# Relative-bias rows made beside the first convolution layer and copied DRAM to DRAM in eight pieces

## The chip, the cores and the metric

The kernel runs on one core of a Trainium2 chip, as one program from the first load to the last store. The metric is the time of one execution on the device in microseconds (us); of several executions the median is taken.

## The reference, cut to what matters

Two blocks are computed one behind the other for 256 tokens of 1024 features. The first block has two layers: a gated recurrence (HGRN) with a convolutional feed-forward layer behind it, then a sparse attention (DSA) with a second convolutional feed-forward layer behind that. The second block (gMLP, a latent attention, SwiGLU layers) is not touched. What the change is about is the bias of the sparse attention, which depends on the distance between a query and a key:

```
def one_block(args):                      # 128 queries at a time
    scores = where(admissible, index_scores(q_idx, k_idx, w_idx), NEG_BIG)
    _, sel = lax.top_k(scores, top_k)     # the 64 best keys of every query
    logits = q . k[sel] * 64 ** -0.5
    rel = q_pos - sel
    bias = rel_bias[t5_causal_bucket(rel)]   # table of 32 buckets by 16 heads
    probs = softmax(where(rel >= 0, logits + bias, NEG_BIG))
    return probs . v[sel]

def conv_ffn(x, w_up, conv_w, conv_b, w_down):
    h = causal_depthwise_conv3(x @ w_up) + conv_b
    gate, up = split(h)
    return (silu(gate) * up) @ w_down
```

The bias needs nothing that the layers compute: it is made of `rel_bias`, an input, and constants.

## The kernel before

All 256 tokens stay on the chip; weights stream in from DRAM. A **unit** of weights is 1024 rows by 256 columns, 1 MB: `fetch` (L210) issues its load on SP's DMA queue into one of 3 buffers `wst`, `unit` (L227) splits it in two parts whose sum it is (ScalarE writes `whi`, VectorE then `wlo`, 4 buffers each), and TensorE multiplies with `feat` or `tok`, three products for each of the 8 blocks of 128 rows. A load can be issued when the VectorE split of the unit three before has read its buffer, a split when TensorE is done with the unit four before. So the weights run ahead of TensorE by up to three split units and three loaded or loading ones.

`conv_ffn` (L666) runs 11 times over a pair of units, one for the gate and one for the up part: TensorE fills a bank `acc` (4 of them), VectorE scales it into `cvx` (2 buffers), ScalarE and VectorE form the convolution in `cvg` and `cvu`, and the product is split into `fh` and `fl`. Then `down` multiplies with `ffn_w_down`, 12 units.

`rel_bias` (L1041) stands behind the first layer's `conv_ffn` in the program. It loads a one-hot matrix `onehot` (distance to bucket) and the table `rtab`, makes one matrix product into a bank `mx`, copies it to `rrow` in SBUF (head by distance, 384 values in each of 16 rows), and writes every row 128 times to `bias_rows` in DRAM, 3 MB in one transfer. `dsa` (L1059) then reads, for 12 steps, a skewed window of it into `dx` (L1163), to which the products of queries and keys are added. Its weights come as one unit for index keys and keys, two for the index queries `dqi`, half a unit for values and four for queries `dq`; index scores (`pr`, L1106, then `drl`, L1109, then `dsc`) and the 64 best keys (L1122, L1123) come ahead of the 12 steps.

What sets the order of the work is a scheduler of the build: instructions are placed on each engine by modelled readiness, unless `behind` ties them to TensorE's last instruction so far. On an engine, and on SP's queue of DMA issues, they then run strictly in the order so found: a wait of one holds all behind it. Buffers of a tag are handed out in program order (`onehot` and `dx` take from the 4 of tag `e`, which `cvg` uses too; `rrow` from the 4 of tag `m`).

Of the kernel before, what the change touches and what calls it, by code (L numbers as in the profile page):

```python
# [15 lines left out]
P = 128  # L16
# [19 lines left out]
# buffers by tag: a tag's tiles are handed out in the order of the program  # L36
# [9 lines left out]
# a step's later parts, in steps behind its first, and the steps before which the queries' products come  # L46
# [7 lines left out]
# V values, N turned latent of the queries, P their rope part, R its rope, Q queries, S scores, T turned, O out  # L54
MLA_ORDER = "N0 V0 N1 V1 V2 P0 P1 Q0 R0 Q1 R1 S0 Q2 S1 T0 Q3 O0 S2 T1 S3 V3 O1 T2 O2 T3 O3"
TURN_OLD, TURN_NEW = (8, 5), (6, 4)
N_HOLD = 3
N_START = 12
# [63 lines left out]
class Feat:  # L122
    """1024 or more features by 256 tokens, two chunks of 128 features to a tile"""
# [14 lines left out]
class Split:  # L138
    """a Feat in two parts, hi and lo, whose sum it is"""
# [8 lines left out]
class Net:  # L148
# [10 lines left out]
    # ---- tiles  # L159
# [32 lines left out]
    def behind(s):  # L192
        """what follows on TensorE is queued behind the last of its instructions so far"""
        pe = mybir.EngineType.PE
        return s.tc.issue_after(next(i for i in reversed(s.nc.cur_bb.bb.instructions) if i.engine == pe))

    def warm(s, n):
        """n products that nobody reads, behind the last of TensorE's instructions so far: its clock halves at rest"""
        if n:
            with s.behind():  # L200
                ps = s.prod()
                x = s.ident.bitcast(BF16)
                for _ in range(n):
                    s.nc.tensor.matmul(ps[:, :T], x[:, :P], x, start=True, stop=True)

    # ---- weights
    def fetch(s, parts, k0, nk, cuts=1):
        """columns of matrices, side by side, for k of 128 rows: on their way"""
# [14 lines left out]
    def begin(s, p, fine=0):  # L223
        """a layer: the first of its weights are split in smaller pieces"""
        s.fine, s.order = fine or N_FINE, list(ORD_POST if s.posted else ORD_RES)
        s.marks = p.marks

    def unit(s, parts, k0, nk, fetched=None):
        """the same, split in two"""
# [13 lines left out]
        with ExitStack() as stack:  # L243
            # behind what the layer waits for
# [10 lines left out]
    def feat(s, w, c, x, ps):  # L255
        """ps[c-th 128 columns of w, tokens] = w^T x over the unit's k."""
# [10 lines left out]
    def feat2(s, w, x, c=0, beside=None):  # L267
        """two chunks of columns in one bank; beside() after each, in this order on TensorE"""
# [11 lines left out]
    def tok(s, w, cols, t, x, ps, ks=None):  # L280
        """ps[tokens of tile t, cols of w] = x^T w over the unit's k."""
# [11 lines left out]
    def tok2(s, w, x, beside=None):  # L293
        """both tiles of tokens by the 256 columns of a unit, in one bank"""
# [8 lines left out]
    def split_scaled(s, parts):  # L303
        """(hi, lo, source, scale) of several chunks: a tile's parts are all written before they are read"""
# [6 lines left out]
    # ---- norms  # L311
    class Sum:
        """squares summed over chunks; the last chunk is left apart"""

    def sumsq(s, sm, src, k, n, scale=None):
# [3 lines left out]
        if k == n - 4:  # L319
            # the table of the square root, ahead of its use  # L320
# [8 lines left out]
    def rsqrt(s, out, ss, n, eps, factor=1.0):  # L329
        """out = factor * (ss / n + eps) ** -0.5 on small tiles."""  # L330
# [14 lines left out]
    def rsqrt_v(s, out, ss, n, eps):  # L345
        """the same on VectorE alone: a first guess from the bits, then Newton's steps"""
# [13 lines left out]
    def colsum(s, sm, st):  # L360
        """per-token sums of feature-major tiles -> [128 tokens, 2] in a bank"""
# [5 lines left out]
    def bcast(s, r, st):  # L367
        """[128 tokens, 2] -> [128, 256] of a bank, the same on all partitions"""
# [12 lines left out]
    class Pre:  # L381
        """the input of a layer, normed and split: x(k). The token's factor is left to its consumer:
        r by token, rb along the free axis"""
# [8 lines left out]
    def pre_group(s, p, n, sums=True, bank=None):  # L392
        """256 features of h, turned and split, and their squares' sums"""
# [13 lines left out]
    def pre_half(s, p, t, m, sums=True):  # L407
        """the same for a half of the features of a tile of tokens"""
# [15 lines left out]
    def squares(s, ss, src, n):  # L424
        """the sums of squares by token of a group of 256 features, src by token tile"""
# [3 lines left out]
        if n == 2:  # L429
            # the table of the square root, ahead of its use  # L430
# [20 lines left out]
    # ---- start  # L451
    def load_vectors(s, g, parts, queue):
        """rows of 128 values -> one column of s.vectors each"""
# [81 lines left out]
    def conv_vectors(s, l):  # L535
        """the taps and biases of a layer's convolution"""
# [7 lines left out]
    # ---- feed-forward layers  # L544
    def down(s, w, hid, kn, out, n_beside=0):
        """out(n, ps) for the 4 groups of 256 columns of hid @ w, hid of kn chunks; ps by token tile"""
# [4 lines left out]
        for n in range(4 - out.late):  # L551
            both = n < n_beside
            if both:
                # the two tiles in one bank, zeroed for both: a chunk of hid serves both at once
# [25 lines left out]
        # the last units: a tile of tokens to its end, then the other  # L580
# [32 lines left out]
    def tok_turn(s, p, units, t, ps, at=()):  # L613
        """both units side by side for a tile of tokens, what p has left to do before the k's in at"""
# [11 lines left out]
    def swiglu(s, p, wg, wu, wd, out, beside=None):  # L626
# [3 lines left out]
        for i in range(KF // 2):  # L630
# [4 lines left out]
            if p.halves and i == 0:  # L635
                # by token: the first tile of tokens is there before the second
# [26 lines left out]
    def conv_ffn(s, p, l, out):  # L663
# [11 lines left out]
        h2 = lambda x: x.rearrange("p (j t) -> p j t", j=2)  # L675
        for i in range(KF // 2):
            if l == 0 and i in (3, 6):
                # those of the next one
                if i == 3:
                    turns = s.conv_vectors(1)  # L680
                else:
                    with s.behind():
                        for turn in turns:
                            turn()
            ys = [s.e("cvg"), s.m("cvu")]
# [28 lines left out]
    # ---- first block, layer 0  # L714
    def hgrn(s, p, first):
# [40 lines left out]
        def decay(pr):  # L756
            """the logarithms, summed from the start of a chunk"""
# [11 lines left out]
            # exp(x - bk) = k exp(x - b)  # L769
# [4 lines left out]
        def query(pr):  # L774
            """without the tokens' factor"""
# [5 lines left out]
        def offsets():  # L781
            """what lies between a chunk of 32 and the border of the two tiles of 128 tokens"""
# [7 lines left out]
            # the same for the 64 tokens at the start of every 128  # L790
# [13 lines left out]
        def gates(pr):  # L804
            """silu(x) = x / 2 * (1 + tanh(x / 2)); x / 2 without the tokens' factor"""
# [9 lines left out]
        def prepare(pr):  # L815
            """the products' place"""
# [6 lines left out]
        def inner(pr):  # L823
# [4 lines left out]
            def blocks(m, B):  # L828
                """B tokens against the B before them, where these begin at a multiple of 2 B"""
# [8 lines left out]
            def diagonal(lv, x, y):  # L838
                """the pairs of 2^lv tokens, (row of the first half, column of the second)"""
# [8 lines left out]
            # chunks of 32 against the borders between them: keys before a border, queries behind it  # L848
# [39 lines left out]
            # within the chunks, against the middle of every 2 B tokens  # L888
# [61 lines left out]
        # the heads' parts, a few at a time beside the halves of the products  # L950
        def parts():
            steps, at = 0, {}
            for pr in range(NP):
                while len(qs) <= pr:
                    yield
                for _ in inner(pr):
                    # the ends of the pairs before, some steps later
# [82 lines left out]
    # ---- first block, layer 1  # L1040
    def rel_bias(s):  # L1041
        """rows of the bias by distance, in DRAM: for head h and query row q of 128, a row whose
        value 127 - q + j is the bias of the key j - 128 behind the block"""
        nc, a = s.nc, s.a
        onehot = s.e("onehot")[:, :384]
        tab = s.tmp("rtab", P)
        nc.sync.dma_start(onehot, a["consts"][:, C_ONEHOT:])
        nc.gpsimd.memset(tab, 0.0)
        nc.gpsimd.memset(tab[32:64], NEG)
        nc.sync.dma_start(tab[:32, :16], a["rel_bias"])  # L1050
        ps = s.mix()
        nc.tensor.matmul(ps[:, :384], tab, onehot, start=True, stop=True)
        row = s.m("rrow")[:, :384]
        nc.vector.tensor_copy(row, ps[:, :384])
        scr = s.dp.tile([16, P, 384], F32, name="bias_rows")
        nc.sync.dma_start(scr, row[:16][:, None, :].to_broadcast([16, P, 384]))
        s.bias_rows = scr

    def dsa(s, p, out_):  # L1059
# [6 lines left out]
        # index keys and weights beside a filler, then the keys of both heads  # L1066
# [706 lines left out]
```

## Time and profile before

| | |
|---|---|
| median of 3 runs | 1662.58 us (1660.65 to 1665.51) |
| span of the profiled execution, first to last instruction | 1657.0 us |
| median less span: what lies around the span | 5.6 us |
| TensorE busy, share of the span | 98% |
| VectorE, ScalarE, GpSimd busy | 69%, 55%, 0% |
| DMA queue of SP: packets' time, share of 16 engines' span | 57.8% |
| HBM read, written | 291.19 MB, 4.19 MB |

The own time of the profiled execution is not listed beside its span; the median stands for it. TensorE's 98% are counted over overlapping matmuls. In the table of 40 slices only one slice of TensorE's granted clock falls below 9 tenths behind the start of the program, the tenth (373 to 414 us), and its busy digit there is 5. Shares of the span are means over stages with different limits, so the rows below are read by stage: the sparse attention's begin (355 to 420 us) and the first convolution layer (180 to 290 us).

### The profile page before, as it was taken

The numbers are of one execution on the slowest core, as the hardware profiler recorded it, in microseconds if no ns is written. First come the engines' busy times: TensorE is split into PE (matmuls) and PEld (weight loads), VectorE is DVE, ScalarE is ACT, GpSimd is POOL, SyncE is SP. The second block draws the span as 40 slices with busy tenths as digits, with TensorE's granted clock in tenths as the row PEclk, the third lists the DMA queues.
The fourth block names the chain that finished last, engine by engine and source line by source line (L and its number), as shares of the span: only waits on it lengthen the run. The fifth ranks groups of instructions, "written<-read, shape, count | busy, mean of one in ns | idle before, by whom it ended". The sixth has DMA issues, their size and how long they took to land.

```text
span 1657.0 us, 34152 instructions
## 1 busy us (share of the span) xinstructions
PE 1619.9 (98%) x14500; PEld 1606.8 (97%) x14502; DVE 1150.6 (69%) x1900; ACT 913.8 (55%) x1443; POOL 6.7 (0%) x28
## 2 busy tenths in 40 slices
PE   8989999995999999999999999999999999999998
PEld 7989999995999999999999999999999999999998
DVE  6986899654859886766667857664686647677653
ACT  7865766453656656544465546444564446665442
POOL 0000000000000000000000000000000000000000
PEclk9999999997999999999999999999999999999999
DMA  8731755678446566566847565556376565447562
GB/s 266 217 100 53 228 188 187 191 154 190 136 136 218 174 202 192 184 192 193 250 144 228 178 191 172 185 171 203 124 241 188 195 201 142 154 133 227 184 202 71
DMA packets 303821, 297.58 MB, mean 180 GB/s; under 512 B 14295, under 2 KB 300214, under 8 KB 303670
## 3 DMA queue, kind: packets, MB, share of 16 engines
q1 hardware_dynamic: 303622, 295.40, 57.8%
q8 instruction: 114, 1.87, 0.5%
q14 instruction: 37, 0.30, 0.1%
q10 hardware_dynamic: 48, 0.01, 0.0%
HBM read 291.19 MB, written 4.19 MB: 178 GB/s over the span
## 4 chain that ended last, share of the span: by engine, by line
PE 91%; DVE 3%; DMA 3%; ACT 2%; issue 1%; SPq 0%; DVEq 0%; ACTq 0%
PE acc L265 16%; PE acc L263 16%; PE acc L264 16%; PE acc L565 8%; PE acc L567 7%; PE acc L566 7%; PE acc L289 3%; PE acc L290 3%; PE acc L291 3%; DMA bias_rows<-rrow 2%; PE acc L576 2%; PE acc L578 2%; PE acc L577 1%; DVE wlo L251 1%; ACT whi L249 1%; PE pr L844 1%
## 5 line engine op out<-in xcount | busy, mean ns | idle before, releaser
L249 ACT ACTIVATE whi<-wst 128x2048 fp32r<-128x2048 f32 (+4 forms) x404 | 524.2, 1331 | 507.1 <-issue 225.3
L251 DVE TENSOR_TENSOR wlo<-wst,whi 128x2048 fp32r<-128x2048 f32 (+4 forms) x404 | 620.9, 1560 | 247.4 <-ACT whi L249 245.6
L263 PE MATMUL acc<-xh,whi 128*128 128x256 f32 x2416 | 671.9, 279 | 1.3 <-ACT xh L306 0.9
L264 PE MATMUL acc<-xl,whi 128*128 128x256 f32 x2416 | 671.8, 279 | 1.0 <-DVE xl L308 1.0
L265 PE MATMUL acc<-xh,wlo 128*128 128x256 f32 x2416 | 671.3, 279 | 0.5 <-DVE wlo L251 0.5
L264 PEld LDWEIGHTS acc<-xl,whi 128*128 128x128 f32 x2416 | 456.1, 189 | 1.7 <-DVE xl L308 1.4
L263 PEld LDWEIGHTS acc<-xh,whi 128*128 128x128 f32 x2416 | 453.4, 188 | 2.0 <-ACT xh L306 1.1
L265 PEld LDWEIGHTS acc<-xh,wlo 128*128 128x128 f32 x2416 | 454.2, 188 | 0.9 <-DVE wlo L251 0.7
L567 PE MATMUL acc<-wlo,fh 128*128 128x256 f32 x880 | 245.0, 279 | 0.0
L566 PE MATMUL acc<-whi,fl 128*128 128x256 f32 x880 | 244.1, 278 | 0.0
L565 PE MATMUL acc<-whi,fh 128*128 128x256 f32 x880 | 244.0, 278 | 0.0
L567 PEld LDWEIGHTS acc<-wlo,fh 128*128 128x128 f32 x880 | 165.2, 188 | 0.0
L566 PEld LDWEIGHTS acc<-whi,fl 128*128 128x128 f32 x880 | 165.1, 188 | 0.0
L565 PEld LDWEIGHTS acc<-whi,fh 128*128 128x128 f32 x880 | 164.9, 188 | 0.0
L289 PE MATMUL acc<-whi,xh 128*128 128x256 f32 x384 | 108.9, 283 | 0.0
L290 PE MATMUL acc<-whi,xl 128*128 128x256 f32 x384 | 107.0, 279 | 0.0
L291 PE MATMUL acc<-wlo,xh 128*128 128x256 f32 x384 | 107.0, 279 | 0.0
L289 PEld LDWEIGHTS acc<-whi,xh 128*128 128x128 f32 x384 | 72.1, 188 | 0.2
L290 PEld LDWEIGHTS acc<-whi,xl 128*128 128x128 f32 x384 | 72.1, 188 | 0.0
L291 PEld LDWEIGHTS acc<-wlo,xh 128*128 128x128 f32 x384 | 72.1, 188 | 0.0
L658 DVE TENSOR_TENSOR ffu<-acc,rb 128x512 f32<-128x512 f32 x41 | 28.3, 690 | 46.5 <-PE acc L265 46.4
L308 DVE SCALAR_TENSOR_TENSOR xl<-mx,vectors,xh 128x128 fp32r<-128x128 f32 (+1 forms) x124 | 39.1, 375 | 22.9 <-ACT xh L306 22.8
(422 smaller groups left out, 2116.6 us busy)
## 6 DMA issues: line engine op xcount, KB each, us to landing
wst<-in_ffn_w_up_dram SPq DMA_DIRECT2D x88, 1024.0 KB, 5.3
wst<-in_ffn_w_down_dram SPq DMA_DIRECT2D x48, 1024.0 KB, 5.4
wst<-in_ffn_w_gate_dram SPq DMA_DIRECT2D x44, 1024.0 KB, 5.4
wst<-in_ffn_w_down_dram SPq DMA_DIRECT2D x24, 768.0 KB, 4.8
wst<-in_gmlp_w_in_dram SPq DMA_DIRECT2D x16, 1024.0 KB, 5.6
wst<-in_hgrn_w_in_dram SPq DMA_DIRECT2D x13, 1024.0 KB, 5.7
wst<-in_gmlp_w_out_dram SPq DMA_DIRECT2D x8, 1024.0 KB
wst<-in_dsa_w_in_dram SPq DMA_DIRECT2D x6, 1024.0 KB
```

What stands on the lines that cost most here:

```text
L249: s.nc.scalar.activation(hi[:, c], w[:, c], AF.Copy)
L251: s.nc.vector.tensor_tensor(lo[:, c], w[:, c], hi[:, c].bitcast(F32), op=OP.subtract)
L263: mm(ps, wh[:, k, cols], xh, start=k == 0, stop=False)
L264: mm(ps, wh[:, k, cols], xl, start=False, stop=False)
L265: mm(ps, wl[:, k, cols], xh, start=False, stop=k == nk - 1)
L289: mm(ps, xh[:, ts], wk, start=k == 0, stop=False)
L290: mm(ps, xl[:, ts], wk, start=False, stop=False)
L291: mm(ps, xh[:, ts], lk, start=False, stop=k == nk - 1)
L308: b = s.nc.vector.scalar_tensor_tensor(lo, src, g, hi.bitcast(F32), op0=OP.mult, op1=OP.subtract)
L565: mm(ps[t], xh, wh[:, k], start=k0 + k == 0 and not both, stop=False)
L566: mm(ps[t], xl, wh[:, k], start=False, stop=False)
L567: mm(ps[t], xh, wl[:, k], start=False, stop=k0 + k == kn - 1 and (t == 1 or not both))
```

## The change

`rel_bias` now returns a list of ten steps instead of running at once, and `conv_ffn` of the first layer takes one of them from the list at each of its passes 1 to 10, ahead of the pass's products. The first step loads `onehot` and `rtab`. The second makes the product, tied behind TensorE's last instruction, copies 16 rows of it to `rrow`, and writes them once to `bias_row` in DRAM (24 KB). The other eight each copy two heads' rows from `bias_row`, 128 times each, to `bias_rows`, DRAM to DRAM (384 KB written). The call behind `conv_ffn` goes. The rest of the file's difference is comments.

```
+N_SPREAD = 2
...
         h2 = lambda x: x.rearrange("p (j t) -> p j t", j=2)
+        bias = s.rel_bias() if l == 0 else []
         for i in range(KF // 2):
...
+            if i and bias:
+                bias.pop(0)()
             ys = [s.e("cvg"), s.m("cvu")]
...
     def rel_bias(s):
         nc, a = s.nc, s.a
-        onehot = s.e("onehot")[:, :384]
-        tab = s.tmp("rtab", P)
-        nc.sync.dma_start(onehot, a["consts"][:, C_ONEHOT:])
-        nc.gpsimd.memset(tab, 0.0)
-        nc.gpsimd.memset(tab[32:64], NEG)
-        nc.sync.dma_start(tab[:32, :16], a["rel_bias"])
-        ps = s.mix()
-        nc.tensor.matmul(ps[:, :384], tab, onehot, start=True, stop=True)
-        row = s.m("rrow")[:, :384]
-        nc.vector.tensor_copy(row, ps[:, :384])
+        flat = s.dp.tile([16, 384], F32, name="bias_row")
         scr = s.dp.tile([16, P, 384], F32, name="bias_rows")
-        nc.sync.dma_start(scr, row[:16][:, None, :].to_broadcast([16, P, 384]))
         s.bias_rows = scr
+        parts = []
+
+        def load():
+            onehot, tab = s.e("onehot")[:, :384], s.tmp("rtab", P)
+            nc.sync.dma_start(onehot, a["consts"][:, C_ONEHOT:])
+            nc.gpsimd.memset(tab, 0.0)
+            nc.gpsimd.memset(tab[32:64], NEG)
+            nc.sync.dma_start(tab[:32, :16], a["rel_bias"])
+            parts.extend((onehot, tab))
+
+        def product():
+            onehot, tab = parts
+            with s.behind():
+                ps = s.mix()
+                nc.tensor.matmul(ps[:, :384], tab, onehot, start=True, stop=True)
+            row = s.m("rrow")[:, :384]
+            nc.vector.tensor_copy(row[:16], ps[:16, :384])
+            nc.sync.dma_start(flat, row[:16])
+
+        def spread(h):
+            nc.sync.dma_start(scr[h:h + N_SPREAD], flat[h:h + N_SPREAD][:, None, :].to_broadcast([N_SPREAD, P, 384]))
+
+        return [load, product] + [lambda h=h: spread(h) for h in range(0, 16, N_SPREAD)]
...
         s.conv_ffn(p, 0, s.residual(nxt))
-        s.rel_bias()
```

Where the scheduler puts this is seen in the built programs. Lines of the changed file have other numbers than those of the file before.

SP's queue of DMA issues, before, from the last weights of the recurrence to the first of `down`:

```order
L216 DMA wst<-in_hgrn_w_out_dram 128x8x256 x4
L216 DMA wst<-in_ffn_w_up_dram 128x8x256 x3
L1050 DMA rtab<-in_rel_bias_dram 32x16
L216 DMA wst<-in_ffn_w_up_dram 128x8x256 x19
L216 DMA wst<-in_ffn_w_down_dram 128x6x256
```

The same queue in the changed kernel, from the fourth unit of `ffn_w_up`:

```order
L218 DMA wst<-in_ffn_w_up_dram 128x8x256 x4
L1057 DMA onehot<-in_consts_dram 128x384
L218 DMA wst<-in_ffn_w_up_dram 128x8x256 x4
L1070 DMA bias_row<-rrow 16x384
L1073 DMA bias_rows<-bias_row 256x1x384 x3
L218 DMA wst<-in_ffn_w_up_dram 128x8x256
L1073 DMA bias_rows<-bias_row 256x1x384 x5
L218 DMA wst<-in_ffn_w_up_dram 128x8x256 x10
```

The eight pieces stand not one to a pass but in two groups, three between the eleventh and the twelfth unit of `ffn_w_up` and five between the twelfth and the thirteenth. The first waits for the landing of `bias_row`.

SP's queue where the sparse attention begins, before:

```order
L216 DMA wst<-in_dsa_w_in_dram 128x8x128
L216 DMA wst<-in_dsa_w_in_dram 128x8x256 x2
L1056 DMA bias_rows<-rrow 2048x1x384
L216 DMA wst<-in_dsa_w_in_dram 128x8x256
L1163 DMA dx<-bias_rows 128x4x128 x4
L216 DMA wst<-in_dsa_w_in_dram 128x8x256
L216 DMA wst<-in_dsa_w_out_dram 128x8x256 x3
```

And now:

```order
L218 DMA wst<-in_dsa_w_in_dram 128x8x128
L218 DMA wst<-in_dsa_w_in_dram 128x8x256 x3
L1181 DMA dx<-bias_rows 128x4x128 x4
L218 DMA wst<-in_dsa_w_in_dram 128x8x256
L218 DMA wst<-in_dsa_w_out_dram 128x8x256 x3
```

The 3 MB transfer is gone from between the query units; the four `dx` loads stand where they stood, ahead of the last query unit.

VectorE in the convolution layer, ahead of the split of the ninth unit of `ffn_w_up` (the `wlo` row), before:

```order
L690 TENSOR_TENSOR cvx<-acc,rb 128x512
L672 SCALAR_TENSOR_TENSOR cvg<-cvx,vectors,cvg 128x255
L673 SCALAR_TENSOR_TENSOR cvg<-cvx,vectors,cvg 128x254
L251 TENSOR_TENSOR wlo<-wst,whi 128x2048
L301 TENSOR_TENSOR fl<-cvu,fh 128x512
```

And now:

```order
L695 TENSOR_TENSOR cvx<-acc,rb 128x512
L674 SCALAR_TENSOR_TENSOR cvg<-cvx,vectors,cvg 128x255
L675 SCALAR_TENSOR_TENSOR cvg<-cvx,vectors,cvg 128x254
L1069 COPY rrow<-mx 16x384
L253 TENSOR_TENSOR wlo<-wst,whi 128x2048
```

The copy to `rrow` has come in just ahead of that split; on TensorE the product stands behind the fourth unit of the layer.

## Rows read from the trace of the kernel before

**Rows 1.** The page: its span, and the chain that ended last by engine.
```profile
span 1657.0 us, 34152 instructions
...
PE 91%; DVE 3%; DMA 3%; ACT 2%; issue 1%; SPq 0%; DVEq 0%; ACTq 0%
```

**Rows 2.** Chain in order of time, 340 to 460 us: start us, us, what.
```profile
355.64 32.54 DMA bias_rows<-rrow
...
390.31 7.64 DMA wst<-in_dsa_w_in_dram
```

**Rows 3.** Timelines of SP, ACT, DVE there: start us, us, instruction, [idle before <-releaser].
```profile
356.41 9.46 SPq L216 DMA_DIRECT2D wst<-in_dsa_w_in_dram  x1
...
391.47 1.91 ACT L249 ACTIVATE whi<-wst 128x2048 fp32r<-128x2048 f32 x1 [20.37 <-DMA wst<-in_dsa_w_in_dram]
...
400.00 2.29 DVE L251 TENSOR_TENSOR wlo<-wst,whi 128x2048 fp32r<-128x2048 f32 x1 [2.88 <-ACT whi L249]
```

**Rows 4.** Stretches: PE, PEld, DVE, ACT, POOL busy us (count), PEclk, DMA share, GB/s.
```profile
377.40:393.70 16.30, 0.28 (x3) 0.07 (x1) 0.29 (x1) 2.23 (x3) 0.00 (x0) 0.58 0.99 188
393.70:397.30 3.60, 3.60 (x17) 3.60 (x18) 3.25 (x5) 0.22 (x1) 0.00 (x0) 0.52 1.11 339
...
405.00:419.20 14.20, 14.15 (x119) 13.73 (x118) 13.82 (x56) 7.91 (x12) 0.00 (x0) 1.00 0.14 48
sum 41.80, PE 24.72 PEld 23.61 DVE 22.19 ACT 14.87 POOL 0.00; mean PE 4.94 PEld 4.72 DVE 4.44 ACT 2.97 POOL 0.00
```

**Rows 5.** Timeline of SP, convolution layer: loads of its eleventh and twelfth units.
```profile
198.04 0.37 SPq L216 DMA_DIRECT2D wst<-in_ffn_w_up_dram  x1
202.62 0.37 SPq L216 DMA_DIRECT2D wst<-in_ffn_w_up_dram  x1
```

**Rows 6.** Timelines of ACT (twelfth, thirteenth unit) and DVE (ninth, twelfth): the splits.
```profile
214.31 1.92 ACT L249 ACTIVATE whi<-wst 128x2048 fp32r<-128x2048 f32 x1
219.75 1.92 ACT L249 ACTIVATE whi<-wst 128x2048 fp32r<-128x2048 f32 x1 [2.54 <-PE acc L264]
...
200.31 2.28 DVE L251 TENSOR_TENSOR wlo<-wst,whi 128x2048 fp32r<-128x2048 f32 x1
...
216.27 2.29 DVE L251 TENSOR_TENSOR wlo<-wst,whi 128x2048 fp32r<-128x2048 f32 x1
```

**Rows 7.** A stretch of the convolution layer, columns as in the stretches above.
```profile
195.00:215.00 20.00, 20.00 (x179) 20.00 (x178) 19.52 (x29) 13.11 (x17) 0.00 (x0) 1.00 0.72 225
```

**Rows 8.** DMA view, 116 to 121 us, one load of a unit; page: units' landing.
```profile
DMA packets 1041, 1.07 MB, mean 213 GB/s; under 512 B 16, under 2 KB 1040, under 8 KB 1040
...
q1 hardware_dynamic: 1040, 1.05, 64.9%
...
wst<-in_ffn_w_up_dram SPq DMA_DIRECT2D x88, 1024.0 KB, 5.3
```

**Rows 9.** DMA view, 1645 to 1657 us: the eight stores of the result, SBUF to DRAM.
```profile
q1 hardware_dynamic: 1152, 1.05, 26.2%
...
out_dram<-h SPq DMA_DIRECT2D x8, 128.0 KB, 1.8
```

**Rows 10.** DMA view, 358 to 387 us: the transfer to bias_rows alone.
```profile
q1 hardware_dynamic: 1934, 2.97, 89.9%
```

**Rows 11.** DMA view, 74 to 81 us: four loads of 44 rows, one unit landing.
```profile
DMA packets 1793, 1.70 MB, mean 243 GB/s; under 512 B 60, under 2 KB 1792, under 8 KB 1792
...
vst<-in_ffn_conv_w_dram SPq DMA_DIRECT2D x3, 22.0 KB
vst<-in_ffn_conv_b_dram SPq DMA_DIRECT2D x1, 22.0 KB
```

**Rows 12.** Page: the queue of ACT's DMAs; DMA view 0 to 2.2 us: its two loads.
```profile
q10 hardware_dynamic: 48, 0.01, 0.0%
...
vst<-in_attn_norm_dram ACTq DMA_DIRECT2D x1, 8.0 KB
vst<-n_hgrn_lower_bounds_dram ACTq DMA_DIRECT2D x1, 4.0 KB
```

More of the change, by code (lines that the diff above doesn't have):

```diff
@@ L312 @@
     class Sum:
+        pass
     def sumsq(s, sm, src, k, n, scale=None):
@@ L381 @@
     class Pre:
+        pass
     def pre(s, gain):
```

## The prediction

> **What bounds the kernel now.** The first view is the page with its chain of the work that ended last: 91% of the span is TensorE, 3% (some 50 us) a DMA [rows 1]. A kernel that waits for TensorE nearly everywhere gains only where TensorE stands still, so the second view is the chain in order of time: one transfer, `bias_rows`, holds it for 32.5 us, and behind it a unit of weights for another 7.6 [rows 2]. Third, the timelines there: the query unit whose load SP issued at 356.41 was on the same DMA queue behind the 3 MB, the issue itself took 9.46 us where such an issue else takes 0.37 [rows 5], and ScalarE's split of it stood 20.37 us until 391.47, with everything behind it on ScalarE [rows 3]. So a transfer of a queue lands after those ahead of it. Fourth, the table of stretches: TensorE is idle from 377.4 to 393.7, its granted clock falls to half (1.2 of 2.4 GHz) and stays at 0.52 for another 3.6 us of work [rows 4].
>
> **What it removes.** From 377.4 to 419.2 there are 41.8 us with 24.7 us of TensorE's work [rows 4], of which 3.6 at half clock would take 1.8 at full: 22.9 us are needed, so 18.9 us go if TensorE is fed throughout. VectorE had 22.2 us of work there, also less than that; from 405 on both were full, so neither hides more. The bounds: 16.0, from 377.4 to 393.4, the hole alone, if the restart stays as it is; 20.4, ScalarE's whole wait, if all behind it, VectorE's split of the last query unit at 400.00 too [rows 3], moves up by as much. The four `dx` loads still stand ahead of the last query unit on SP; they take buffers of the layers before, free when ScalarE came free before (391.47 - 20.37 = 371.1). I take 18.9. The product, the copy and the small loads only move.
>
> **What it adds.** Eight pieces, 3.15 MB in all, DRAM to DRAM, on the queue that feeds the convolution layer. First their price. The trace has no DRAM to DRAM transfer. A unit of 1.05 MB from DRAM took 64.9% of 16 engines for 5 us, 52 us of engine time [rows 8]; the result's 1.05 MB into DRAM 26.2% of 12 us, 50 us [rows 9]. The transfer that goes took 89.9% of 29 us for 2.97 MB, 147 us of engine time for 1.05 MB [rows 10], three times as much, but its source was sixteen rows of SBUF, which the pieces don't read. I take 50, as both directions show it: 150 us of engine time for all pieces, 18.8 a piece; the far end is 55 a piece.
>
> Then on how many engines. A transfer ends with one small packet on each engine that it ran on: one unit's load, 128 rows, shows 16 packets under 512 B [rows 8]. Four loads of 44 rows beside one unit's landing show 60, so 44 for the four, 11 each [rows 11]. The loads of 16 and of 8 rows that ScalarE issued have 48 packets: 24 of data and 24, 16 and 8 [rows 12]. The number of engines is thus the largest up to 16 that divides the rows: 11 for 44, 8 for 8. A piece has 256 rows where it lands but two where it is read, each read 128 times; by the first it runs on 16 engines, by the second on two. In none of these rows does an engine get less than a whole row of the source, so I take **two engines**. The transfer that goes (16 rows read, 2048 written) doesn't tell. The Trainium skill (DMA: Bandwidth & Descriptors, Why a DMA increments its semaphore by 16 and not by 1) says that the number must divide the slowest dimension on both sides; by it a piece has two engines, by a rule of the target alone sixteen, and the sums are the two below. The rows on loads of 44, 16 and 8 rows agree with it, but their two sides are alike.
>
> Two engines: 9.4 us a piece, 75 us for eight. The other 14 engines are free, but a unit of weights lands only when its parts on those two have.
>
> Now when. `rrow` is copied just ahead of the ninth unit's split, which begins at 200.3 [rows 6]; `bias_row` is issued near 201, behind the eleventh unit's load, issued at 198.04 [rows 5] and landing 5.3 us later [rows 8]. SP waits for it to about 203.8. With the start of a small transfer (it lands 1.8 us after its issue, [rows 9]) the first piece moves at about 205. Three pieces: 233.2. The twelfth unit's part, 50 / 16 = 3.1 us, and half a us to tell of it: 236.9 instead of 208. Its split takes 4.25 us (214.31 to 218.56, [rows 6]): 241.1.
>
> When is it due? The thirteenth unit's split waited to 219.75 for TensorE's end with the ninth, of which it takes the buffer, and units follow each other in 5.44 us [rows 6]. So TensorE begins the twelfth at 219.75 + 2 x 5.44 = 230.6. **First stop: 10.5 us.** The thirteenth unit stands behind five more pieces: 236.4 + 47.0 + 3.1 + 0.5 + 4.25 = 291.3; due at 241.1 + 5.44 = 246.5. **Second stop: 44.8 us.** The next units land 3 us apart behind it, in time.
>
> Each stop has a restart at half clock, as the one of before had: 1.8 us each, 3.6. And VectorE is 98% busy in this layer [rows 7]; what it has left over from the units before the stop it can't catch up until `down`, where TensorE then waits for the last part of the hidden features: I put 4 us, between none and the 8 that its work on some three units would be, less the splits. Sum: 10.5 + 44.8 + 3.6 + 4 = 62.9 lost, 18.9 won, **44 us more**. The span is 1657.0, the median 5.6 above it; with the same around it, 1701 of span and 1706 of time. The look-ahead of the weights (28 us from the twelfth's issue to its use) has been taken off once: that is the cover, and it is used up in the first stop.
>
> Low end: wider packets (1536 B rather than 1024) may cost less for each byte; 8 us a piece (64 in all), no late catching up and 20.4 won make 6.3 + 37.7 + 3.6 - 20.4 = 27 more, 1690. High end within two engines: a third more for reading and writing DRAM at once, 12.5 us a piece, the stops 19.8 and 60.2, 1731.
>
> **The rivals.**
> *Sixteen engines.* Then a piece takes 1.2 us, all eight 9.4. The twelfth unit lands at 205 + 3.5 + 3.6 = 212, ahead of its split at 214.31, the thirteenth near 218, ahead of 219.75: no stop, 18.9 us won, **1644, faster**. For it: the target's 256 rows, and the scheduler may carry the split of either side. Against it: the rows on loads of 44 and 8. It turns on one number: with four engines (37.5 us) the first stop vanishes, the second is 291.3 - 37.7 - 236.1 = 17.5, and with its restart the change is worth nothing, 1663. Above four it wins.
> *The price of the old transfer.* If writing rows of 1536 B to DRAM in this form, and not the sixteen rows of SBUF, made the old transfer slow, a piece takes 27.5 us on two engines, 220 for all, 145 more than above: **1851**. Against it: the stores of the result at a third of that price.
> *The pieces apart.* If they really were one to a pass, 9.4 us each against a unit's 3.1 us twice in 10.9, the two engines would still have 15.6 us of work in each 10.9: a loss of about 8 x 4.7 - 28, some 10 us, less the 18.9 won: 1654. The order of SP's queue shows two groups instead, and it runs in that order.
>
> **How the numbers follow.** Two engines at about the price of rows 8 and 9: 0.84, likeliest 1706, its own range 1690 to 1731. Old price: 0.03. Sixteen engines or eight: 0.10. Four engines, or a copy so cheap that it balances: 0.03. The range 1686 to 1733 holds nearly all of the first case, 0.81 of the whole, and leaves the others out. Slower by over 0.3% (5 us, about what a measurement of this kernel can tell from no change): 0.87; within it 0.03; faster 0.10.
>
> **What would show it.** In the changed kernel's stretch 200 to 300 us: a DMA share near 2/16 for tens of us, ScalarE's `whi` waiting for `in_ffn_w_up` twice, TensorE idle for some 10 and then 45 us with its clock at half; a few small packets for each piece, two and not sixteen. At the attention's begin: no hole, no `bias_rows` in the chain, the units from `dqi` to the first `dx` closer by 19 us. It is wrong if the pieces pass at 300 GB/s with the weights undisturbed (sixteen engines), or if TensorE stands longer than 70 us (price).

## The result and the profile after

| | before | after |
|---|---|---|
| median | 1662.26 us (4 runs, 1660.65 to 1665.51) | 1684.90 us (4 runs, 1680.10 to 1691.04) |
| profiled execution: time, span | not listed, 1657.0 us | 1680.1 us, 1678.3 us |

The ratio is 1.0137, 95% interval 1.0098 to 1.0175: slower by 22.6 us, where 44 were predicted, and 1.1 us below the low end of the range. The sign, the two engines and the two stops came out; the size didn't. In every listed run the time is 1.8 us above the span (2.1 in e7), so most of the 5.6 us that the table of the kernel before puts around its span will be that its profiled execution was faster than the median.

The page of the kernel after, the rows that answer to [rows 1], with the group of matmuls that waited most (columns: busy us, mean ns | idle before, releaser):

```profile
span 1678.3 us, 34157 instructions
...
PE 92%; DVE 2%; SPq 2%; DMA 1%; ACT 1%; issue 1%; DVEq 0%; ACTq 0%
...
L265 PE MATMUL acc<-xh,whi 128*128 128x256 f32 x2416 | 673.5, 280 | 39.7 <-DVE cvx L695 38.9
```

`bias_rows` has left the chain as a transfer (before it was 32.54 us of it, [rows 2]); in its place stand SP's issues of the pieces and a load of `ffn_w_up`. The chain in order of time, 214 to 282 us (start us, us, what):

```profile
221.95 4.37 SPq L1073
...
232.88 7.75 SPq L1073
...
240.68 7.73 SPq L1073
...
248.45 7.73 SPq L1073
...
256.29 18.18 DMA wst<-in_ffn_w_up_dram
...
274.56 1.92 ACT whi L251
...
278.71 0.68 DVE cvx L695
```

The pieces follow each other at 7.75 us, not 9.4. The thirteenth unit's load, issued at 256.29, lands 18.18 us later, behind what is left of them. ScalarE's two waits for such a unit, in its timeline (last column: idle before, releaser):

```profile
232.38 1.91 ACT L251 ACTIVATE whi<-wst 128x2048 fp32r<-128x2048 f32 x1 [16.58 <-DMA wst<-in_ffn_w_up_dram]
...
274.56 1.91 ACT L251 ACTIVATE whi<-wst 128x2048 fp32r<-128x2048 f32 x1 [39.28 <-DMA wst<-in_ffn_w_up_dram]
```

And TensorE's two stops:

```profile
237.97 0.46 PE L265 MATMUL acc<-xh,whi 128*128 128x256 f32 x1 [4.83 <-DVE cvx L695]
...
279.54 0.55 PE L265 MATMUL acc<-xh,whi 128*128 128x256 f32 x1 [34.05 <-DVE cvx L695]
```

The releaser named is VectorE's `cvx`, not the unit. VectorE works in order: the split `wlo` of the late unit stands ahead of the `cvx` that empties a bank `acc`, so the late unit holds back both, and the bank came last, 0.7 us behind the split.

The stretches of the kernel after (columns as in [rows 4]):

```profile
233.00:238.00 5.00, 0.17 (x3) 0.06 (x1) 3.67 (x4) 2.28 (x3) 0.00 (x0) 1.00 0.13 50
238.00:245.50 7.50, 7.49 (x50) 7.25 (x50) 1.40 (x4) 0.00 (x0) 0.00 (x0) 0.77 0.14 53
245.50:279.50 34.00, 0.00 (x0) 0.00 (x0) 3.00 (x3) 4.01 (x6) 0.00 (x0) 0.54 0.39 130
279.50:283.00 3.50, 3.46 (x18) 3.49 (x19) 3.50 (x9) 2.82 (x3) 0.00 (x0) 0.58 0.90 286
283.00:295.00 12.00, 11.90 (x102) 11.73 (x101) 12.00 (x18) 8.34 (x10) 0.00 (x0) 1.00 0.58 181
295.00:337.60 42.60, 42.60 (x364) 42.60 (x363) 42.60 (x63) 29.95 (x36) 0.00 (x0) 1.00 0.58 187
401.20:433.00 31.80, 31.80 (x266) 31.33 (x265) 20.72 (x41) 16.99 (x30) 0.00 (x0) 1.00 0.72 224
```

While only pieces pass, the DMA share is 0.13 to 0.14 at 50 GB/s. Behind each stop the granted clock is at its lower level (1.2 of 2.4 GHz) for a while: a mean of 0.77 over 7.5 us and 0.58 over 3.5 is 3.5 and 2.9 us at half, so 1.7 and 1.5 us lost. The last row is the attention's begin, which answers to [rows 4]: TensorE full at full clock, the hole gone.

Where the stages begin, in TensorE's timelines, first `down` of the layer, first product of the attention, first `down` of the attention. Before:

```profile
290.42 0.28 PE L264 MATMUL acc<-xl,whi 128*128 128x256 f32 x1
290.53 0.28 PE L265 MATMUL acc<-xh,wlo 128*128 128x256 f32 x1
290.64 0.28 PE L565 MATMUL acc<-whi,fh 128*128 128x256 f32 x1
...
353.51 0.28 PE L263 MATMUL acc<-xh,whi 128*128 128x256 f32 x1
...
447.82 0.47 PE L565 MATMUL acc<-whi,zh 128*128 128x256 f32 x1
```

And after:

```profile
337.41 0.28 PE L266 MATMUL acc<-xl,whi 128*128 128x256 f32 x1
337.53 0.28 PE L267 MATMUL acc<-xh,wlo 128*128 128x256 f32 x1
337.65 0.28 PE L567 MATMUL acc<-whi,fh 128*128 128x256 f32 x1
...
401.18 0.28 PE L265 MATMUL acc<-xh,whi 128*128 128x256 f32 x1
...
475.33 0.47 PE L567 MATMUL acc<-whi,zh 128*128 128x256 f32 x1
```

The layer ends 47.0 us later. The attention, from its first product to its `down`, takes 74.15 us instead of 94.31: 20.2 won. From there to the end the kernel after takes 1203.0 us, before 1209.2, with the same program: the section on the hardware has what this is.

### The profile page after: what moved, and what is told of

Its sections match the earlier page's. It is cut to its first block, busy times and chain, and to the rows that moved or that the text cites. A ratio compares the mean times of both kernels' runs of the same rounds, so it can differ in the third digit from the quotient of the medians.

```text
span 1678.3 us, 34157 instructions
## 1 busy us (share of the span) xinstructions
PE 1620.0 (97%) x14500; PEld 1607.1 (96%) x14502; DVE 1150.2 (69%) x1900; ACT 913.1 (54%) x1443; POOL 6.8 (0%) x28
## 4 chain that ended last, share of the span: by engine, by line
PE 92%; DVE 2%; SPq 2%; DMA 1%; ACT 1%; issue 1%; DVEq 0%; ACTq 0%
PE acc L265 16%; PE acc L267 16%; PE acc L266 16%; PE acc L567 7%; PE acc L569 7%; PE acc L568 7%; PE acc L291 3%; PE acc L292 3%; PE acc L293 3%; SPq L1073 2%; PE acc L580 1%; PE acc L578 1%; PE acc L579 1%; DMA wst<-in_ffn_w_up_dram 1%; ACT whi L251 1%; PE pr L849 1%
```

## The experiments

Theory A: the stops come of the number of engines, and that is the number of rows that a piece reads (two). Its rivals: B, such a copy passes at 50 GB/s whatever the engines; C, each piece has a fixed price; D, the old transfer was slow because of its place or its writing, not its source. A later group asks what holds the units back: the engines, the queue, or the issue. All times below are medians, ratios are to the kernel before, with the 95% interval.

**e1: sixteen rows of source.**

```diff
-nc.sync.dma_start(scr[h:h + N_SPREAD], flat[h:h + N_SPREAD][:, None, :].to_broadcast([N_SPREAD, P, 384]))
+nc.sync.dma_start(scr[:, h:h + 16], flat[:, None, :].to_broadcast([16, 16, 384]))
...
-[lambda h=h: spread(h) for h in range(0, 16, N_SPREAD)]
+[lambda h=h: spread(h) for h in range(0, P, 16)]
```

> Eight pieces as in the changed kernel, at the same places and of the same 384 KB, but each takes 16 query rows of all 16 heads, so that its source has 16 rows and not two. Theory A (the stops come of two engines, because the source of a piece has two rows, and a packet of 1536 B takes an engine some 61 ns): a piece takes 16 engines 1 us, all eight 7.75; the twelfth unit lands near 212, ahead of its use, no stop, and the 20.2 us that the attention's begin gained (401.18 to 475.33, before 353.51 to 447.82) stay: 1662.3 - 20.2 = 1642 us. Rival B (a DRAM to DRAM copy that reads few rows again and again runs at some 50 GB/s whatever the engines): 62 us for all, as in the changed kernel, 1685. Rival C (each piece costs a fixed 7.75 us): 1685 too.

Measured: 1640.9 us, ratio 0.9886 (0.9848 to 0.9924). Its DMA view, 205 to 214 us:

```profile
DMA packets 2070, 2.60 MB, mean 288 GB/s; under 512 B 73, under 2 KB 2069, under 8 KB 2069
```

The same eight pieces in the same places, the same bytes and packets, and 44 us less than the changed kernel: B and C fall, A stands.

**e2: four pieces of four heads; e3: one of sixteen.** One constant:

```diff
-N_SPREAD = 2
+N_SPREAD = 4      (e2; 16 in e3)
```

> Four pieces of four heads each instead of eight of two. SP's queue then holds three between the eleventh and the twelfth unit and one behind the twelfth. Theory A (engines as many as source rows): four engines, 128 packets each, 7.75 us a piece, 31 us for all. First stop as in the changed kernel, 4.8 us, the thirteenth unit lands near 243.5 and TensorE stands some 3 more, with two restarts at half clock 11 in all, against 20.2 won: 1653. The prediction's own price (37.5 us for all, break-even at four engines) said 1663. Rival B (50 GB/s whatever the engines): 62 us, 15.5 a piece, the twelfth unit lands at 255, one stop of some 26 and another of 12: 1682. Rival C (fixed time for each piece) gives the same as A here.

> One piece of all 16 heads, 3 MB, ahead of the twelfth unit. Theory A: 16 engines, 128 packets each, 7.75 us; the twelfth unit lands near 217, its split comes some us later than before and still ahead of its use at 233: no stop, 1642. Rival B (50 GB/s whatever the engines): 62 us ahead of the twelfth unit, which lands at 271: one stop of 43 us, about 1688. Rival C: as A.

Measured: e2 1654.7 us, ratio 0.9963 (0.9939 to 0.9987); e3 1640.7 us, 0.9872 (0.9833 to 0.9911). TensorE's waits in e2, 195 to 320 us (total us, times, longest), e2's queue from 208 to 216 us, while only pieces pass (packets, MB, share of 16 engines), then ScalarE's split of the twelfth unit in e3 and e3's DMA view, 208 to 214 us:

```profile
PE acc L265 <- DVE cvx L695: 8.7, 2, 7.3
```

```profile
q1 hardware_dynamic: 504, 0.77, 26.2%
```

```profile
224.03 1.91 ACT L251 ACTIVATE whi<-wst 128x2048 fp32r<-128x2048 f32 x1 [9.19 <-DMA wst<-in_ffn_w_up_dram]
```

```profile
DMA packets 1099, 1.69 MB, mean 282 GB/s; under 512 B 0, under 2 KB 1098, under 8 KB 1098
```

Two, four and sixteen engines: 1685, 1655, 1641; two rows had a share of 0.13, four have 0.26. In e2 the stops are 7.3 and 1.4 us, not 4.8 and 3, and a third of 1.3 behind `fh` makes 10.0 where 7.8 were expected. In e3 the twelfth unit came at 224, not 217: on 16 engines the copy ran at 282 GB/s, 18 an engine, where two engines did 25 each. The layer's loads were not the reason: 1.69 MB in 1099 packets are 1538 B each, so these are packets of the copy alone. Still in time, so it cost nothing.

In all these runs the rows that a transfer reads are also the heads that it writes. That the source side sets the number rests on the listing of SP's queue, where the target of a piece is one block of 256 rows; no run sets the two apart.

**e4: two rows to a packet, still two engines.** `bias_row` holds each row twice:

```diff
...
-nc.sync.dma_start(flat, row[:16])
+nc.sync.dma_start(flat.rearrange("h (j c) -> h j c", j=2), row[:16][:, None, :].to_broadcast([16, 2, 384]))
...
-nc.sync.dma_start(scr[h:h + N_SPREAD], flat[h:h + N_SPREAD][:, None, :].to_broadcast([N_SPREAD, P, 384]))
+nc.sync.dma_start(scr[h:h + N_SPREAD].rearrange("h (q j) c -> h q (j c)", j=2),
+                  flat[h:h + N_SPREAD][:, None, :].to_broadcast([N_SPREAD, P // 2, 768]))
```

> Eight pieces of two heads on two engines as in the changed kernel, the same bytes at the same places, but bias_row holds each row twice, so that one packet carries 3072 B (two query rows) and there are 64 a piece and engine, not 128. Theory A1 (the price is by bytes, 61 ns for 1536 B and so some 120 for 3072): 62 us for all, unchanged, 1685. Theory A2 (the price is by packet, 61 ns whatever its size up to there): 31 us for all; the twelfth unit lands near 220, in time, the thirteenth near 243, a stop of some 3 and one restart: 1647.

Measured: 1688.1 us, ratio 1.0150 (1.0116 to 1.0185). Its DMA view, 225 to 245 us, and that of the changed kernel, 235 to 255:

```profile
DMA packets 429, 1.05 MB, mean 53 GB/s; under 512 B 6, under 2 KB 134, under 8 KB 428
```

```profile
DMA packets 659, 1.02 MB, mean 51 GB/s; under 512 B 4, under 2 KB 658, under 8 KB 658
...
q1 hardware_dynamic: 658, 1.00, 13.3%
```

Fewer packets (3072 B instead of 1536 B), the same rate: the price is by bytes between these two sizes, 25 GB/s an engine. 13.3% of 16 engines is 2.1, though two were at work: packets of one engine overlap.

**e5: the old place, but DRAM to DRAM; e6: the new place, but from SBUF.** In e5, against the kernel before:

```diff
...
-nc.sync.dma_start(scr, row[:16][:, None, :].to_broadcast([16, P, 384]))
+nc.sync.dma_start(flat, row[:16])
+nc.sync.dma_start(scr, flat[:, None, :].to_broadcast([16, P, 384]))
```

In e6, against the changed kernel (the pieces go):

```diff
...
-nc.sync.dma_start(flat, row[:16])
+nc.sync.dma_start(scr, row[:16][:, None, :].to_broadcast([16, P, 384]))
...
```

> The kernel before, with its bias rows still made and written behind the first layer, but in two steps: 16 rows once to DRAM (24 KB), then one transfer DRAM to DRAM on 16 rows of source in the place of the one from SBUF. Theory A (the price of the old transfer is its source in SBUF; DRAM to DRAM on 16 engines takes 7.75 us as in e3): the transfer is 24.8 us shorter, less some 2 us until the first step has landed; the query unit behind it lands ahead of the time at which ScalarE comes free (371.1), no hole, 1662 - 19 to 20 = 1642: the move into the convolution layer is not needed. Rival D (what made the old transfer slow is where it stood, among the attention's loads, or its writing): 27 to 32 us as before and 1660.

> The changed kernel with the old transfer: made beside the first convolution layer, but written in one transfer from 16 rows of SBUF, ahead of the twelfth unit, no pieces. Theory A (32.5 us wherever it stands): the twelfth unit lands near 203.5 + 32.5 + 3.6 = 239.6 rather than by 228, is split by 244, TensorE was due at 233: a stop of some 11 us and one restart of 1.7, against 20.2 won: 1655. Rival D (it is the place that made it slow): some 8 us, no stop, 1642. If the look-ahead covers it all: 1642 too, with the transfer at 32 us in the trace.

Measured: e5 1644.4 us, ratio 0.9907 (0.9877 to 0.9937); e6 1653.1 us, 0.9960 (0.9940 to 0.9981). The DMA views while the transfer runs, e5 359 to 369 us and e6 206 to 232, and TensorE's wait in e6:

```profile
DMA packets 2665, 3.63 MB, mean 363 GB/s; under 512 B 16, under 2 KB 2664, under 8 KB 2664
```

```profile
DMA packets 1721, 2.66 MB, mean 102 GB/s; under 512 B 0, under 2 KB 1719, under 8 KB 1719
...
q1 hardware_dynamic: 1719, 2.64, 90.5%
```

```profile
PE acc L265 <- ACT fh L302: 11.0, 1, 11.0
```

D falls: from 16 rows of SBUF it is 102 GB/s in either place ([rows 10]: the same in the old one), from DRAM 363 (the end of a unit's load among it) in the old place, with TensorE full from 355 to 415 us. So nearly the whole gain is had by the source alone, without the move: at the attention's `down` e5 is 18.0 us ahead of the kernel before (429.80 against 447.82), e3 18.6 (429.21). The move alone, with a stop of 11.0 us, keeps 8 of the 20. The 7.75 us that e5's expectation gives for e3 were the reckoned time; at 282 GB/s e3's 3.15 MB take 11.

**e7: GpSimd's queue; e10: ScalarE's queue.** The pieces of the changed kernel, two rows of source each, off SP's queue:

```diff
-nc.sync.dma_start(scr[h:h + N_SPREAD], ...)
+nc.gpsimd.dma_start(scr[h:h + N_SPREAD], ...)     (e7)
+with s.tc.issue_after(s.last_act()):              (e10: one to a pass, behind ScalarE's last instruction so far)
+    nc.scalar.dma_start(scr[h:h + N_SPREAD], ...)
```

> The eight pieces of the changed kernel on two engines each, issued by GpSimd on a queue of its own and not by SP, so that units of weights don't stand behind them. Theory E (the two engines are what is short, and serve both queues in turn): while the pieces pass, a unit lands only every 7.4 us or so (65 packets on each of those engines, each beside one of 61 ns), the pieces end some 116 us after the first, TensorE needs 86 to 89 for the units of that time, and the look-ahead of 28 covers the difference: hardly a stop, 1645. Rival F (the same bytes on the same two engines cost the same whoever issues them): stops of some 39, 1685.

> The same eight pieces (two rows of source each), one to a pass, issued on ScalarE's DMA queue in ScalarE's order, not on SP's, so that no unit stands behind them in its queue. In e7 GpSimd's queue carried them at up to 160 GB/s and more, so it didn't use two engines, and its 1644 us don't tell queue from engines; this run does. Theory E: the trace shows some 50 GB/s more beside the units and no more, about two engines; a piece takes 7.75 us of both, with two units 13.3 of each 10.9 to 11.3 us, within the look-ahead: no stop, 1641 to 1645. Rival I (the issue of a piece holds the issuing engine, as SP was held 8 us by its third piece): ScalarE's splits come late by up to 8 us each, stops of tens of us, 1665 or more. Rival J (a queue of its own spreads the pieces over more engines, as GpSimd's did): each piece some 1 to 3 us long, 1641.

Measured: e7 1643.9 us, ratio 0.9915 (0.9881 to 0.9949); e10 1651.0 us, 0.9937 (0.9917 to 0.9957). The queues' rows, e7 from 205 to 225 us and e10 from 200 to 300 (packets, MB, share of 16 engines), and in e10 ScalarE's last two issues with work behind them, and TensorE's wait:

```profile
q0 software_dynamic: 4437, 2.90, 62.8%
```

```profile
q10 hardware_dynamic: 1491, 2.27, 6.0%
```

```profile
288.35 4.99 ACTq L1078 DMA_DIRECT2D bias_rows<-bias_row  x1
...
299.73 6.74 ACTq L1078 DMA_DIRECT2D bias_rows<-bias_row  x1
...
306.52 1.10 ACT L677 ACTIVATE cvu<-cvx,vectors 128x256 f32<-128x256 f32 x2 [5.49 <-issue]
...
312.37 1.91 ACT L255 ACTIVATE whi<-wst 128x2048 fp32r<-128x2048 f32 x1 [2.43 <-DMA wst<-in_ffn_w_down_dram]
314.18 0.61 ACT L306 ACTIVATE fh<-cvu 128x512 fp32r<-128x512 f32 x1
```

```profile
PE acc L571 <- ACT fh L306: 6.5, 1, 6.5
```

e7 met its number for another reason than E's: the pieces used 10 of 16 engines' time in these 20 us and were nearly through in them, not in 116. They were also cut otherwise: 4437 packets for 2.90 MB are 654 B on the mean, not 1536, so e7 changes more than the queue. The Trainium skill (DMA: Bandwidth & Descriptors, Why a DMA increments its semaphore by 16 and not by 1) has a rule by which this would come out: a hardware queue always takes the lowest-numbered engines, GpSimd's takes the next ones in turn for each transfer. No row here names the engines, so this fits and isn't shown. In e10 the pieces behave as on SP's queue (nearly six of them, 96 us of engine time, so 16 each) and the units pass beside them without a stop up to 300 us, as E says. Then ScalarE's last two issues take 5.0 and 6.7 us, and its work behind the second begins 5.5 us late, as rival I says. TensorE's one stop, 6.5 us, ends with `fh` at 314.18, and `fh` stands on ScalarE behind the split of a unit that had only just landed, 13.64 us after its issue. So the last link of that stop is a late unit, which is E's side of it, though E had no stop; what the held issue has in it isn't shown. J falls.

**e8: one piece ahead of each unit; e9: ahead of each second one.** Each piece is tied behind SP's last load, the next load behind it, from the twelfth unit on:

```diff
+if bias and 2 * i + (first > 0) >= 11:               (e8; e9 does it in fetch, at even units)
+    with s.tc.issue_after(s.last_load()):
+        bias.pop(0)()
+    with s.tc.issue_after(s.last_load()):
+        got = s.fetch(part, 0, KD)
```

> The eight pieces of the changed kernel (two engines, SP's queue), one ahead of each of the units twelve to nineteen, instead of three and five. Theory E (engine time decides): each piece with its unit takes the queue 10.9 us where TensorE needs 5.5 to 5.65; the nineteenth unit lands near 293 and TensorE stands some 27 us in several short stops, with up to 8 for restarts at half clock; 20.2 won: 1671 to 1678. The prediction's rival (apart they are nearly covered): 1654 or less.

> The same eight pieces on two engines, SP's queue, one ahead of every second unit from the twelfth on (six in the rest of the convolution layer, two among the first units of the layer's down product). In e8 a piece and a unit took the queue 10.5 us, so a unit alone 2.8. Theory E (engine time against the look-ahead): a piece and two units take 13.3 us where TensorE needs 10.9 to 11.3; 2 to 2.4 us are lost on each piece, 16 to 19 in all, less than the look-ahead of 28: no stop, and with the 20 won 1641 to 1645. Rival H (a piece ahead of a unit stops TensorE, whatever the distance to the next): stops as in e8 or half of them, 1655 to 1671. The prediction's sum for this case, with 9.4 us a piece, was 1654.

Measured: e8 1671.3 us, ratio 1.0077 (1.0048 to 1.0106); e9 1654.0 us, 0.9949 (0.9931 to 0.9967). ScalarE's splits behind a piece, in e8 and in e9:

```profile
238.47 1.92 ACT L255 ACTIVATE whi<-wst 128x2048 fp32r<-128x2048 f32 x1 [4.57 <-DMA wst<-in_ffn_w_up_dram]
249.04 1.92 ACT L255 ACTIVATE whi<-wst 128x2048 fp32r<-128x2048 f32 x1 [8.13 <-DMA wst<-in_ffn_w_up_dram]
```

```profile
219.70 1.92 ACT L264 ACTIVATE whi<-wst 128x2048 fp32r<-128x2048 f32 x1 [4.10 <-DMA wst<-in_ffn_w_up_dram]
...
260.18 1.92 ACT L264 ACTIVATE whi<-wst 128x2048 fp32r<-128x2048 f32 x1 [5.99 <-DMA wst<-in_ffn_w_up_dram]
...
273.66 1.92 ACT L264 ACTIVATE whi<-wst 128x2048 fp32r<-128x2048 f32 x1 [5.91 <-DMA wst<-in_ffn_w_up_dram]
```

In e8 a piece and a unit take 10.5 us where TensorE needs 5.65, as expected. In e9 E missed by 10 us. The pace is as expected (13.5 us for a piece and two units, against 11.3), but the cover wasn't 28: the twelfth unit was split at 219.70 and TensorE was due with it near 233, with 4.25 us of splitting ahead of that, so about 9 us were left behind the first piece. At 2.2 a pass they are gone after four, at 273.66. From 260 to 320 us TensorE is idle 10.5 us in the stretches, and a restart follows. The 28 us counted the unit's own landing and split, and the piece itself, as cover.

## Why the prediction was right, and where its size failed

| term, us | predicted | profiled execution after |
|---|---|---|
| first stop | 10.5 | 4.8 |
| second stop | 44.8 | 34.1 |
| restarts at half clock | 3.6 | 3.2 |
| late catching up, other | 4 | about 1 |
| slower cadence of matmuls in this layer | none | about 4 |
| `down`, up to the attention | none | 0.7 |
| attention's begin | -18.9 | -20.2 |
| the rest of the program | none | -6.2 |
| sum | +44 | +21.3 of span |

**Right.** Where TensorE stood, and that the hole goes without a remainder: ScalarE's whole wait went, as the upper bound of 20.4 had it, 20.2; e1, e3 and e5 end at 1641 to 1644 on this alone. Two engines, from loads whose two sides were alike ([rows 11, 12]): the share of 0.13 and e1 to e3 show it, and so do the small packets that it named as a sign: 4 under 512 B in the changed kernel's 235 to 255 us (the second of e4's views), two for each of the two pieces that end there. The queue: two groups, two stops, both followed by half clock. The rival of sixteen engines, with 1644 for its time, is e1 with 1641; it was a forecast of another kernel. The Trainium skill's rule on the number of engines that the prediction names (DMA: Bandwidth & Descriptors, Why a DMA increments its semaphore by 16 and not by 1) agrees with the runs on SP's queue: a share of 0.13 with two rows of source, 0.26 with four.

**The step that failed is the price of a piece**, 9.4 us from 50 us of engine time for 1.05 MB. Measured are 7.75 us for 0.39 MB on two engines, 41 us for 1.05 MB. Over eight pieces this is 13.2 of the 19.8 us by which the first three rows and the catching up were too long. [Rows 8 and 9] gave the sum of the packets' times, and that counts an engine twice where its packets overlap; [rows 4] show it, a share of 1.11. The rate was the better measure: a unit's load at its height in the view of before,

```profile
GB/s 382 389 396 382 382 348 362 362 348 375 382 375 307 150 55 27 20 14 0 0 0 0 0 0 0 0 20 102 137 116 102 184 321 369 341 396 355 403 389 382
```

moves some 375 GB/s on 16 engines (its first twelve slices), 23 an engine, which is 8.4 us a piece. What makes a piece cheaper still isn't shown: e4 finds nothing in packets of 3072 B against 1536 B, and 1536 B against the load's 1024 B wasn't tried. The prediction's low end had 8 us a piece and no catching up and still came to 27 us: its stops are 5.1 us longer than the measured ones, 2 of them by the price and most of the rest because both stops began later than reckoned (below).

Without the two rows that come of the cadence of the matmuls (this layer's, and the rest of the program), the measured terms make 23.6 us, near the 22.6 of the medians.

**The first stop** is smaller by 5.0 for three pieces at 1.65 less, and was due 2.5 us later, at 233.1, since TensorE's units took 5.65 us here and not 5.44; the bank's `cvx` behind the split took 1.4 back. **The second** is 11.8 earlier at its end and 1.0 earlier at its beginning. Between the two stops TensorE took 7.5 us for its unit (237.97 to 245.49), not 5.44, and 1.7 of them are the first restart at half clock: the sum counts that restart as a loss and leaves it out of the time at which the second stop begins, so it is in there twice. **The catching up** of VectorE didn't come to `down`: from 283 us on both engines were full, and VectorE's two units take 9.96 us (its `cvx` pairs stand at 296.21 and 306.17), TensorE's 11.3, so the backlog was worked off in the layer.

**The break-even** said four engines, at 37.5 us for all pieces: e2 with 31 us is 6 us below the kernel before. **The pieces one to a pass** were put at 1654 and e9 is 1654, but by two errors that cancel: a piece costs less and the cover is less.

**What stays open:** why a copy from DRAM on 16 engines runs at 282 GB/s alone in e3's place and the queue at 363 in e5's, which engines GpSimd's queue took, and why a piece costs 7.75 us and not 8.4.

## What to carry to other kernels

Ahead of a transfer with a repeated source, count the rows on its smaller side: on SP's queue here that number, up to 16, was the number of engines (on ScalarE's, two rows behaved alike), and the same bytes cut by query rows instead of by heads made 44 us of difference. A transfer that only ran in the background of another stage is paid by that stage's look-ahead, and only what is left of it after the next unit's own landing and split counts as cover. Take an engine's price from the rate at its height, not from the sum of packet times; and before a slow transfer is moved, try its source: e5, three lines at the old place, gets nearly all that the best of these kernels (e3, 1640.7) has.

## What the runs showed of the hardware

**Two cadences of the same matmuls at the same granted clock.** The starts of successive matmuls stand 0.11 us apart in the rows at 290.42 and 0.12 in those at 337.41. In stretches, before:

```profile
225.00:275.00 50.00, 50.00 (x443) 50.00 (x442) 49.19 (x74) 33.29 (x40) 0.00 (x0) 1.00 0.60 187
...
1100.00:1150.00 50.00, 50.00 (x427) 50.00 (x426) 27.01 (x22) 20.68 (x19) 0.00 (x0) 1.00 0.60 192
```

and after:

```profile
1100.00:1150.00 50.00, 50.00 (x444) 50.00 (x443) 33.25 (x28) 22.06 (x20) 0.00 (x0) 1.00 0.59 190
```

443 or 444 in 50 us, or 427: 4% at a granted clock of 1.00. Each mostly lasts for some tens to two hundred microseconds, and which one a layer has differs between the profiled executions (the first layer has the fast one before, the slow one after, 364 in the 42.6 us from 295 to 337.6). This is about 4 us against the changed kernel in the first layer and some 6 for it behind the attention. From the attention's `down` to the end, which none of the edits touches, the twelve profiled executions take 1203, 1209 or 1215 us, in steps of 6 (1203.0 after, 1209.2 before, 1215.2 in e5). So a few us between medians need not be the change, and up to that `down` e1, e3, e5 and e7 are alike, 18.0 to 19.2 us ahead of the kernel before. It is a likely part of why runs of one kernel lie some 10 us apart, but that isn't shown: there is one profile of each kernel. What chooses the cadence wasn't found.

**An issue can hold its engine.** SP's issue of a piece took up to 8 us (7.7 once three were queued), ScalarE's 5.0 and 6.7 in e10, where an issue of a unit's load takes 0.37 [rows 5]; on an engine that also computes, the work behind it begins late, 5.5 us in e10.
